# Moving two groups of SBUF tiles by 96 bytes, and reordering the products of the output projections

## The chip, the core and the metric

The program runs on one core of one Trainium2 chip, as one launch. The metric is the device time of that launch in microseconds (us), the median of several executions. One further execution is taken under the hardware profiler; all views of the profile come from that one, and the times in them count from the start of its span.

## What is computed

One layer of a transformer-like network on 256 tokens of width 2048, batch 1, all in 32-bit floats: a SwiGLU block, a token mixer, a second SwiGLU block. Each is entered through a layer norm modulated by an "ada" vector, and left through a gated residual and a layer norm:

```python
ada = (jax.nn.silu(c) @ w_ada + b_ada)[:, None, :]
sh1, sc1, g1, sh2, sc2, g2, sh3, sc3, g3 = jnp.split(ada, N_ADA, axis=-1)
h = _swiglu(_modulate(x, sh1, sc1), ffn1_w_in, ffn1_w_out)
x = _layernorm(ALPHA * x + 0.5 * (1 + g1) * h, ln1_g, ln1_b)
h = _token_mixer(_modulate(x, sh2, sc2), w_in, ...)
x = _layernorm(ALPHA * x + (1 + g2) * h, ln2_g, ln2_b)
h = _swiglu(_modulate(x, sh3, sc3), ffn2_w_in, ffn2_w_out)
x = _layernorm(ALPHA * x + 0.5 * (1 + g3) * h, ln3_g, ln3_b)
```

`_swiglu(h, w_in, w_out)` is `(silu(gate) * up) @ w_out` with 5632 features. The mixer multiplies its normalised rows by `w_in` (2048 by 6160), runs eight heads of softmax attention ("fox" heads) and four recurrent heads ("mLSTM"), joins their outputs to rows of width 2048, and multiplies these by its own `w_out`.

## The kernel before

**Products in parts.** Every large product is made of float32r matmuls. Both operands are split (`split`, lines L145 and L146): ScalarE (ACT) casts to a high part `hi`, and VectorE (DVE) subtracts to get a low part `lo`. Three matmuls then stand for one product: high by high, and the two mixed ones. Before the change they all come from `mm3` (L390 to L393). In the trace a matmul is named `out<-moving,stationary`: the stationary operand is loaded first (a weight load, engine row PEld), and then the moving operand streams past it.

**Two forms.** In form a (`cols_form_a`: tiles `s`, `gu_f`, `fh`, `fs`, `pr_m`, `pr_f`) the activations move, 256 columns at a time, and the weights are stationary. L391 and L392 use a weight's high part and L393 its low part. In form b (`mo`, `b_fv`, `b_mv`, `gf`, and the output projections `o_f` and `o_mx`) the weights move, mostly 512 columns at a time, and the activations are stationary: L391 high by high, L392 low weights, L393 low activations.

**Where the tiles lie.** Pools hand out SBUF by offset; a `gap` is a filler tile that does nothing but shift what is allocated after it. In the built program the operands of these matmuls start at these bytes of each partition, given modulo 512:

| operand | before | after |
|---|---|---|
| weights, high parts `hi` (six buffers) | 288 | 288 |
| weights, low parts `lo` (six buffers) | 160 | 160 |
| normalised rows of both SwiGLU blocks, `xhi_f`, `xlo_f` | 480 | 480 |
| normalised rows of the mixer, `xhi_mx`, `xlo_mx` | 384 | 480 |
| hidden rows of the SwiGLU output projections, `hh`, `hl` | 160 | 160 |
| fox heads' rows of the mixer's projection, `yhi`, `ylo` | 64 | 160 |
| mLSTM heads' rows of it, `yh`, `yl` | eight places | the same eight |

After the change `xhi_mx` has the same place as `xhi_f` modulo 8192 too, and `yhi` the same as `hh` modulo 2048.

**Output projections.** `out_proj` runs three times: for the two SwiGLU blocks (`o_f`, 44 row blocks) and for the mixer (`o_mx`, 16). It goes through the 2048 output columns in passes of 1024, 512 and 512, over all row blocks `k` in each, for two tiles of 128 tokens (`a`) and one or two banks of 512 columns (`b`). In the steady state each `k` comes from `load_w` as a pair `(hi, lo)` and is used at once. `held` and `kept` are row blocks whose products are put off to the end of a pass, so that the sums can be taken up by DVE (`add_up`) while PE works on the other token tile. The last four row blocks of the last pass run in halves of 256 columns (`last_products`).

**The order around it.** The tile framework orders each engine's instructions at build time. Beside the weight products it places the generators in `side`: the fox heads (L1075 to L1104) and the mLSTM heads, small chains that go from PE to DVE to ACT and back to PE. A weight goes DMA (issued on SyncE's queue) to `raw` (three buffers), ACT to `hi` (six buffers), DVE to `lo` (six buffers), PE. The ada rows arrive on the same queue and are summed by DVE (L158, L160), at rates set by `pump`.

Of the kernel before, what the change touches and what calls it, by code (L numbers as in the profile page):

```python
# [14 lines left out]
P = 128  # L15
# [32 lines left out]
def layer_kernel(  # L48
# [8 lines left out]
    V, S, G_, PE, SP = nc.vector, nc.scalar, nc.gpsimd, nc.tensor, nc.sync  # L57
# [5 lines left out]
    def gap(pool, nbytes, name):  # L63
        pool.tile([P, nbytes // 4], F32, tag=name, name=name)
# [325 lines left out]
    def mm3(o, ah, al, bh, bl, start, stop):  # L390
        PE.matmul(o, ah, bh, start=start, stop=False)  # L391
        PE.matmul(o, ah, bl, start=False, stop=False)  # L392
        return PE.matmul(o, al, bh, start=False, stop=stop)  # L393
# [28 lines left out]
    def out_proj(w, rows, nk, tag, npump, finish, before=None, turn=0, nheld=3, spare=None):  # L422
# [11 lines left out]
        for width in (1024, 512, 512):  # L434
            nb, kn = width // 512, 2048 // width
            nu = nk // kn
            ps = {(a, b): mm_tile(f"o_{tag}{col}{a}{b}") for b in range(nb) for a in range(2)}
            lastg = col + width == D
            held, kept, last, half = [], [], [], {}

            def products(a, args, k0=turn, k1=(turn - 1) % nk, outs=ps, c=0, w=512):
                ts_ = slice(a * P, (a + 1) * P)
                for k, hh, hl, hi, lo in args:
                    for b in range(nb):
                        bs = slice(b * 512 + c, b * 512 + c + w)
                        mm = mm3(outs[a, b][:, c:c + w], hh[:, ts_], hl[:, ts_], hi[:, bs], lo[:, bs],
                                 k == k0, k == k1)
                return mm


# [1 line left out]
            def last_products(a):  # L452
                half[a, 0] = mm_tile(f"oh_{tag}{a}")
                args = held[:-kn] + (kept if a else []) + held[-kn:]
                k0 = args[0][0] if a and kept and nu == nheld + 1 else None
                body, end = args[:-4], args[-4:]
                ends = end[0][0], end[-1][0]
                with tc.issue_after(last[0].ins) if a else nullcontext():
                    products(a, body, k0, None)
                    products(a, end, None, ends[1], w=256)  # L460
                    last.append(products(a, end, *ends, outs=half, c=256, w=256))


            def add_up(a, ps=ps, col=col, bs=range(nb), half=half):
# [17 lines left out]
            for i in range(nu):  # L482
                u = (i + turn // kn) % nu
                hs = []
                if before:
                    before(u * kn)
                if lastg and nu == 4 and i == nu - 1:
                    catch_up(4)
                keep = spare and lastg and i == nu - nheld - 1
                place, rows_ = spare() if keep else (None, rows)  # L490
                for k in range(u * kn, u * kn + kn, 2):
                    hs += rows_(k)
                for kk, hi, lo in load_w(w[u * kn * P:(u + 1) * kn * P, col:col + width], kn, width,
                                         f"{tag}o{col}_{u}", place):
                    arg = (u * kn + kk, *hs[kk], hi, lo)
                    if keep:
                        products(0, [arg])
                        kept.append(arg)
                    elif lastg and i >= nu - nheld or not lastg and i == nu - 1:
                        held.append(arg)  # L500
                    else:
                        for a in range(2):
                            products(a, [arg])
                if not lastg and i == nu - 1:

                    late += [add_up(a, bs=(b,)) for b in range(nb) for a in range(2)]
                    products(0, held)
                    catch_up(2)
                    products(1, held)
                elif nu > 4:  # L510
                    catch_up(2)
                elif not lastg:
                    catch_up(3)
                if not lastg or i < nu - 4:
                    npump()
# [180 lines left out]
    xp = tc.alloc_tile_pool(name="xp1", bufs=1, **right)  # L696
# [109 lines left out]
    held = {}  # L806
# [68 lines left out]
    for j in range(4):  # L875
        fa = next_ada(j + 1) if j < 3 else load_mixer_smalls()
        for n, i in enumerate(order_of(j)):
            w = list(ws if n + j == 0 else first_w(j, i))
# [8 lines left out]
    lnp = tc.alloc_tile_pool(name="ln1", bufs=1, **right)  # L887
# [17 lines left out]
    ent = {}  # L905

    def finish1(products, add_up, st):
        need(6)
        hp.release()
        ent["xp"] = tc.alloc_tile_pool(name="xp2", bufs=1)  # L910
        gap(ent["xp"], 544, "gap_x")
        ent["np"] = tc.alloc_tile_pool(name="np2", bufs=1)
        ent["f"] = (products, add_up, st)

# [30 lines left out]
    xp, npool = ent["xp"], ent["np"]  # L945
# [326 lines left out]
    for j in range(2):  # L1272
        ps = form_a_pair(C_MQ + j * 256, C_MK + j * 256, f"m{j}")
# [13 lines left out]
    for j in (2, 3, 0, 1):  # L1287
        ps = form_a_pair(C_FQ + j * 256, C_FK + j * 256, f"f{j}")
# [10 lines left out]
    lnp = tc.alloc_tile_pool(name="ln2", bufs=1)  # L1299
# [7 lines left out]
        if len(units) in (8, 12):  # L1307
            need(9 if len(units) == 8 else 10)

    gap(lnp, 224, "gap_y")  # L1310
    yhi, ylo = (lnp.tile([P, NFH, T], F32R, name=f"y{i}") for i in ("hi", "lo"))


# [42 lines left out]
    xp, npool = ent["xp"], ent["np"]  # L1356
# [33 lines left out]
    for j in range(2, 10):  # L1390
# [7 lines left out]
        ps = half_in(j, 0, "fh")  # L1398
# [82 lines left out]
```

## Time and profile before

| | |
|---|---|
| median of three executions | 1930.63 us (1930.4 to 1932.44) |
| the profiled execution, its own time | 1933.45 us |
| its span in the profile | 1931.8 us |
| granted TensorE clock | 0.998 of full speed |
| PE busy in the span | 1882.0 us |
| matmul records | 13109 |

The stages, one after another, from PE's instructions:

| stage | from, us | to, us |
|---|---|---|
| first SwiGLU, in-projection (`s`, `gu_f`) | 38.6 | 530.9 |
| its output projection (`o_f`) | 530.9 | 776.8 |
| mixer: output gates (`mo`) | 776.8 | 831.4 |
| mixer: values (`b_fv`, `b_mv`) | 831.4 | 902.6 |
| mixer: queries and keys (`pr_m`, `pr_f`) | 902.6 | 1059.3 |
| mixer: last values (`b_fv`) | 1059.3 | 1085.5 |
| mixer: output projection (`o_mx`) | 1085.5 | 1185.1 |
| second SwiGLU, in-projection | 1185.1 | 1678.7 |
| its output projection (`o_f`) | 1678.7 | 1931.8 |

A matmul's record has a start and a modelled end, and the records overlap: a matmul of 256 columns is listed with about 0.28 us and one of 512 with about 0.39 us, while the next one starts long before that. What a matmul costs is therefore read as the step from its start to the next start, over a run of matmuls with nothing else in between.

### The profile page before, as it was taken

The numbers are of one execution on the slowest core, as the hardware profiler recorded it, in microseconds if no ns is written. First come the engines' busy times: TensorE is split into PE (matmuls) and PEld (weight loads), VectorE is DVE, ScalarE is ACT, GpSimd is POOL, SyncE is SP. The second block draws the span as 40 slices with busy tenths as digits, with TensorE's granted clock in tenths as the row PEclk, the third lists the DMA queues.
The fourth block names the chain that finished last, engine by engine and source line by source line (L and its number), as shares of the span: only waits on it lengthen the run. The fifth ranks groups of instructions, "written<-read, shape, count | busy, mean of one in ns | idle before, by whom it ended". The sixth has DMA issues, their size and how long they took to land.

```text
span 1931.8 us, 32165 instructions
## 1 busy us (share of the span) xinstructions
PE 1882.0 (97%) x13109; PEld 1726.2 (89%) x13109; DVE 1466.0 (76%) x1774; ACT 931.4 (48%) x1296; POOL 54.2 (3%) x85
## 2 busy tenths in 40 slices
PE   3999999999999999999999999999999999999997
PEld 3999999999988888598999776999999999988886
DVE  7889979877778899678787787777775654555776
ACT  3554354444354464745664544555444444444562
POOL 1211100000000000000000000000000000000000
PEclk9999999999999999999999999999999999999999
DMA  9988969989799887489778784998777656655552
GB/s 354 356 312 304 332 209 315 327 297 335 267 336 315 274 302 259 154 311 318 266 252 288 282 296 147 324 313 270 236 260 257 226 196 197 228 189 193 196 195 89
DMA packets 295819, 510.89 MB, mean 264 GB/s; under 512 B 10834, under 2 KB 158962, under 8 KB 294648
## 3 DMA queue, kind: packets, MB, share of 16 engines
q1 hardware_dynamic: 287896, 480.53, 73.2%
q0 software_dynamic: 7776, 28.32, 4.2%
q8 instruction: 102, 1.67, 0.4%
q14 instruction: 45, 0.37, 0.1%
HBM read 506.71 MB, written 2.10 MB: 263 GB/s over the span
## 4 chain that ended last, share of the span: by engine, by line
PE 90%; DVE 5%; DMA 3%; ACT 1%; issue 1%; POOL 0%; SPq 0%; DVEq 0%; ACTq 0%; POOLq 0%
PE gu_f L391 8%; PE gu_f L393 8%; PE gu_f L392 8%; PE o_f L391 8%; PE o_f L393 8%; PE o_f L392 8%; PE s L391 4%; PE s L392 4%; PE s L393 4%; PE pr_f L393 2%; PE pr_f L392 2%; PE pr_f L391 2%; PE fh L393 2%; PE fh L392 2%; PE fh L391 2%; PE fs L392 1%
## 5 line engine op out<-in xcount | busy, mean ns | idle before, releaser
L160 DVE SCALAR_TENSOR_TENSOR acc<-ar,csil,acc 128x1024 f32<-128x1024 f32 x240 | 306.9, 1279 | 33.0 <-DMA ar<-in_w_ada_dram 32.6
L391 PE MATMUL s<-xhi_f,hi_s 128*128 128x256 f32 x768 | 213.3, 279 | 1.7 <-ACT xhi_f L325 0.9
L392 PE MATMUL s<-xlo_f,hi_s 128*128 128x256 f32 x768 | 213.0, 278 | 0.1
L393 PE MATMUL s<-xhi_f,lo_s 128*128 128x256 f32 x768 | 212.4, 277 | 0.0
L393 PE MATMUL gu_f<-xhi_f,lo_f2i 128*128 128x256 f32 x768 | 212.0, 276 | 0.0
L392 PE MATMUL gu_f<-xlo_f,hi_f2i 128*128 128x256 f32 x768 | 212.0, 276 | 0.0
L391 PE MATMUL gu_f<-xhi_f,hi_f2i 128*128 128x256 f32 x768 | 212.0, 276 | 0.0
L146 DVE TENSOR_TENSOR lo_f2i<-raw_f2i,hi_f2i 128x1024 fp32r<-128x1024 f32 x96 | 117.6, 1225 | 100.1 <-ACT hi_f2i L145 100.0
L391 PE MATMUL gu_f<-xhi_f,hi_f1i 128*128 128x256 f32 x640 | 176.8, 276 | 0.0
L393 PE MATMUL gu_f<-xhi_f,lo_f1i 128*128 128x256 f32 x640 | 176.7, 276 | 0.0
L392 PE MATMUL gu_f<-xlo_f,hi_f1i 128*128 128x256 f32 x640 | 176.7, 276 | 0.0
L145 ACT CAST hi_f2i<-raw_f2i 128x1024 fp32r<-128x1024 f32 x96 | 100.8, 1050 | 137.5 <-PE gu_f L392 125.5
L145 ACT CAST hi_s<-raw_s 128x1024 fp32r<-128x1024 f32 x96 | 100.2, 1053 | 114.0 <-PE s L392 86.8
L391 PEld LDWEIGHTS s<-xhi_f,hi_s 128*128 128x128 f32 x768 | 144.8, 189 | 2.0 <-ACT xhi_f L325 1.1
L392 PEld LDWEIGHTS s<-xlo_f,hi_s 128*128 128x128 f32 x768 | 145.0, 189 | 0.4 <-DVE xlo_f L327 0.3
L393 PEld LDWEIGHTS s<-xhi_f,lo_s 128*128 128x128 f32 x768 | 144.6, 189 | 0.3 <-DVE lo_s L146 0.3
L392 PEld LDWEIGHTS gu_f<-xlo_f,hi_f2i 128*128 128x128 f32 x768 | 144.2, 188 | 0.1
L391 PEld LDWEIGHTS gu_f<-xhi_f,hi_f2i 128*128 128x128 f32 x768 | 144.2, 188 | 0.1
L393 PEld LDWEIGHTS gu_f<-xhi_f,lo_f2i 128*128 128x128 f32 x768 | 144.2, 188 | 0.0
L145 ACT CAST hi_f1i<-raw_f1i 128x1024 fp32r<-128x1024 f32 x80 | 83.6, 1050 | 114.6 <-PE gu_f L392 80.3
L146 DVE TENSOR_TENSOR lo_f2o<-raw_f2o,hi_f2o 128x1024 fp32r<-128x1024 f32 x86 | 105.3, 1224 | 43.2 <-ACT hi_f2o L145 43.1
L145 ACT CAST hh<-hT 128x512 fp32r<-128x512 f32 x126 | 77.3, 620 | 114.1 <-PE o_f L392 113.8
(490 smaller groups left out, 5406.9 us busy)
## 6 DMA issues: line engine op xcount, KB each, us to landing
ar<-in_w_ada_dram SPq DMA_DIRECT2D x240, 512.0 KB, 5.9
raw_s<-in_ffn_w_in_dram SPq DMA_DIRECT2D x48, 1024.0 KB, 7.3
raw_f2i<-in_ffn_w_in_dram SPq DMA_DIRECT2D x48, 1024.0 KB, 5.1
raw_f1o<-in_ffn_w_out_dram SPq DMA_DIRECT2D x44, 1024.0 KB, 7.8
raw_f2o<-in_ffn_w_out_dram SPq DMA_DIRECT2D x44, 1024.0 KB, 5.1
raw_f1i<-in_ffn_w_in_dram SPq DMA_DIRECT2D x40, 1024.0 KB, 7.7
ar<-in_w_ada_dram POOLq DMA_DIRECT2D x48, 512.0 KB, 6.9
raw_mxo<-in_w_out_dram SPq DMA_DIRECT2D x16, 1024.0 KB, 8.1
```

The costliest lines, as they stand in the source:

```text
L145: S.copy(hi, src)
L146: V.tensor_tensor(out=lo, in0=src, in1=hi.bitcast(F32), op=ALU.subtract)
L160: ins = V.scalar_tensor_tensor(out=acc, in0=raw, scalar=csil[:, k:k + 1], in1=acc, op0=ALU.mult, op1=ALU.add)
L391: PE.matmul(o, ah, bh, start=start, stop=False)
L392: PE.matmul(o, ah, bl, start=False, stop=False)
L393: return PE.matmul(o, al, bh, start=False, stop=stop)
```

## The change

Two fillers grow by 96 bytes each, which moves what is allocated behind them: `gap_x` moves the mixer's normalised rows (and the small tiles of the entry to the mixer, `np2`) from 384 to 480 modulo 512, and `gap_y` moves the fox heads' high and low rows from 64 to 160.

In `out_proj` the helper `products` no longer calls `mm3`. It takes the row blocks in pairs (in the steady state it is called with one at a time), issues for all token tiles and banks the two products that read the weights' high part, and only then the products that read the low part. Number and shapes of the matmuls are the same, 12996 in the program before and after.

```diff
-            def products(a, args, k0=turn, k1=(turn - 1) % nk, outs=ps, c=0, w=512):
-                ts_ = slice(a * P, (a + 1) * P)
-                for k, hh, hl, hi, lo in args:
-                    for b in range(nb):
-                        bs = slice(b * 512 + c, b * 512 + c + w)
-                        mm = mm3(outs[a, b][:, c:c + w], hh[:, ts_], hl[:, ts_], hi[:, bs], lo[:, bs],
-                                 k == k0, k == k1)
+            def products(tiles, args, k0=turn, k1=(turn - 1) % nk, outs=ps, c=0, w=512):
+                for i in range(0, len(args), 2):
+                    each = [(arg, a, slice(a * P, (a + 1) * P), b, slice(b * 512 + c, b * 512 + c + w))
+                            for arg in args[i:i + 2] for a in tiles for b in range(nb)]
+                    for (k, hh, hl, hi, lo), a, ts_, b, bs in each:
+                        o = outs[a, b][:, c:c + w]
+                        PE.matmul(o, hh[:, ts_], hi[:, bs], start=k == k0, stop=False)
+                        PE.matmul(o, hl[:, ts_], hi[:, bs], start=False, stop=False)
+                    for (k, hh, hl, hi, lo), a, ts_, b, bs in each:
+                        mm = PE.matmul(outs[a, b][:, c:c + w], hh[:, ts_], lo[:, bs], start=False, stop=k == k1)
                 return mm
...
-                        for a in range(2):
-                            products(a, [arg])
+                        products((0, 1), [arg])
...
-        gap(ent["xp"], 544, "gap_x")
+        gap(ent["xp"], 640, "gap_x")
...
-    gap(lnp, 224, "gap_y")
+    gap(lnp, 320, "gap_y")
```

The other calls of `products` change only in that `a` becomes `(a,)`.

The first place to look at is PE in the steady state of the first SwiGLU's output projection: one row block `k`, with its weights `hi_f1o_10` and `lo_f1o_10`, the rows `hh` and `hl`, and the four sums `o_f_6136` to `o_f_6139`. Before:

```order
L391 MATMUL o_f_6136<-hi_f1o_10_6186,hh_6180 128x512
L392 MATMUL o_f_6136<-lo_f1o_10_6187,hh_6180 128x512
L393 MATMUL o_f_6136<-hi_f1o_10_6186,hl_6181 128x512
L391 MATMUL o_f_6138<-hi_f1o_10_6186,hh_6180 128x512
L392 MATMUL o_f_6138<-lo_f1o_10_6187,hh_6180 128x512
L393 MATMUL o_f_6138<-hi_f1o_10_6186,hl_6181 128x512
```

The other two sums follow in the same way. After the change, PE at the same place, the whole row block:

```order
L447 MATMUL o_f_6136<-hi_f1o_10_6186,hh_6180 128x512
L448 MATMUL o_f_6136<-hi_f1o_10_6186,hl_6181 128x512
L447 MATMUL o_f_6138<-hi_f1o_10_6186,hh_6180 128x512
L448 MATMUL o_f_6138<-hi_f1o_10_6186,hl_6181 128x512
L447 MATMUL o_f_6137<-hi_f1o_10_6186,hh_6180 128x512
L448 MATMUL o_f_6137<-hi_f1o_10_6186,hl_6181 128x512
L447 MATMUL o_f_6139<-hi_f1o_10_6186,hh_6180 128x512
L448 MATMUL o_f_6139<-hi_f1o_10_6186,hl_6181 128x512
L450 MATMUL o_f_6136<-lo_f1o_10_6187,hh_6180 128x512
L450 MATMUL o_f_6138<-lo_f1o_10_6187,hh_6180 128x512
L450 MATMUL o_f_6137<-lo_f1o_10_6187,hh_6180 128x512
L450 MATMUL o_f_6139<-lo_f1o_10_6187,hh_6180 128x512
```

The four products with the low part have moved behind the eight with the high part; a matmul with `hi` is now mostly followed by another with the same `hi`, and one with `lo` by another with the same `lo`.

The second place is PE at the start of the mixer's output projection. `lps1` are logits of fox head 1 (the second of a pair of heads handled there), `ptp0` is the transpose of the softmax `s0` of head 0, and `yhi` and `ylo` are the first row block's parts. Before:

```order
L1078 MATMUL lps1_11488<-qs1_10980 128x256
L391 MATMUL o_mx000_11519<-hi_mxo0_20_11527,yhi_11515 128x512
L392 MATMUL o_mx000_11519<-lo_mxo0_20_11528,yhi_11515 128x512
L391 MATMUL o_mx001_11521<-hi_mxo0_20_11527,yhi_11515 128x512
L392 MATMUL o_mx001_11521<-lo_mxo0_20_11528,yhi_11515 128x512
L391 MATMUL o_mx010_11520<-hi_mxo0_20_11527,yhi_11515 128x512
L392 MATMUL o_mx010_11520<-lo_mxo0_20_11528,yhi_11515 128x512
L391 MATMUL o_mx011_11522<-hi_mxo0_20_11527,yhi_11515 128x512
L392 MATMUL o_mx011_11522<-lo_mxo0_20_11528,yhi_11515 128x512
L1093 MATMUL ptp0_11560<-ident_79,s0_11473 128x128
L393 MATMUL o_mx000_11519<-hi_mxo0_20_11527,ylo_11516 128x512
L393 MATMUL o_mx001_11521<-hi_mxo0_20_11527,ylo_11516 128x512
```

After:

```order
L1080 MATMUL lps1_11488<-qs1_10980 128x256
L447 MATMUL o_mx000_11519<-hi_mxo0_20_11527,yhi_11515 128x512
L447 MATMUL o_mx001_11521<-hi_mxo0_20_11527,yhi_11515 128x512
L447 MATMUL o_mx010_11520<-hi_mxo0_20_11527,yhi_11515 128x512
L447 MATMUL o_mx011_11522<-hi_mxo0_20_11527,yhi_11515 128x512
L1095 MATMUL ptp0_11560<-ident_79,s0_11473 128x128
L448 MATMUL o_mx000_11519<-hi_mxo0_20_11527,ylo_11516 128x512
L448 MATMUL o_mx001_11521<-hi_mxo0_20_11527,ylo_11516 128x512
L448 MATMUL o_mx010_11520<-hi_mxo0_20_11527,ylo_11516 128x512
L448 MATMUL o_mx011_11522<-hi_mxo0_20_11527,ylo_11516 128x512
L450 MATMUL o_mx000_11519<-lo_mxo0_20_11528,yhi_11515 128x512
L450 MATMUL o_mx001_11521<-lo_mxo0_20_11528,yhi_11515 128x512
```

The four products with `lo_mxo0_20` stood between the logits and the transpose `ptp0`, and now stand behind it: four products are left in that place where there were eight. Elsewhere the order of PE changes only among the projections' own products. On ACT and DVE some casts and subtractions of `hh` and `hl` in the output projections come one place later among those of the weights, and two loads on SyncE's queue change places with ada rows.

More of the change, by code (lines that the diff above doesn't have):

```diff
@@ L458, in last_products @@
                 with tc.issue_after(last[0].ins) if a else nullcontext():
-                    products(a, body, k0, None)
-                    products(a, end, None, ends[1], w=256)
-                    last.append(products(a, end, *ends, outs=half, c=256, w=256))
+                    products((a,), body, k0, None)
+                    products((a,), end, None, ends[1], w=256)
+                    last.append(products((a,), end, *ends, outs=half, c=256, w=256))
             def add_up(a, ps=ps, col=col, bs=range(nb), half=half):
@@ L496, in out_proj @@
                     if keep:
-                        products(0, [arg])
+                        products((0,), [arg])
                         kept.append(arg)
@@ L501, in out_proj @@
                     else:
-                        for a in range(2):
-                            products(a, [arg])
+                        products((0, 1), [arg])
                 if not lastg and i == nu - 1:
                     late += [add_up(a, bs=(b,)) for b in range(nb) for a in range(2)]
-                    products(0, held)
+                    products((0,), held)
                     catch_up(2)
-                    products(1, held)
+                    products((1,), held)
                 elif nu > 4:
```

## The prediction

> **What bounds the kernel now.** I read the page first: busy times, the granted clock, the chain that ended last.
>
> ```profile
> span 1931.8 us, 32165 instructions
> PE 1882.0 (97%) x13109; PEld 1726.2 (89%) x13109; DVE 1466.0 (76%) x1774; ACT 931.4 (48%) x1296; POOL 54.2 (3%) x85
> PEclk9999999999999999999999999999999999999999
> PE 90%; DVE 5%; DMA 3%; ACT 1%; issue 1%; POOL 0%; SPq 0%; DVEq 0%; ACTq 0%; POOLq 0%
> ```
>
> PE is busy for 97% of the span, at full clock in every slice, and carries 90% of the chain. It hardly waits, so the change must be priced by what one matmul takes. The number and shapes of the matmuls stay as they are; what can change is the step from one matmul's start to the next. The second view is therefore PE's timeline. I took runs of matmuls with nothing else between them, and divide the distance from the first start to the last by the number of steps. First the form with 256 moving columns, at one place that the change leaves alone and at two that it moves:
>
> ```profile
> 1427.39 0.28 PE L391 MATMUL gu_f<-xhi_f,hi_f2i 128*128 128x256 f32 x1
> ...
> 1574.21 0.28 PE L393 MATMUL gu_f<-xhi_f,lo_f2i 128*128 128x256 f32 x1
> 998.62 0.47 PE L391 MATMUL pr_f<-xhi_mx,hi_f3b 128*128 128x256 f32 x1
> ...
> 1015.65 0.28 PE L393 MATMUL pr_f<-xhi_mx,lo_f0a 128*128 128x256 f32 x1
> ...
> 1046.16 0.37 PE L391 MATMUL pr_f<-xhi_mx,hi_f1b 128*128 128x256 f32 x1
> ...
> 1057.72 0.28 PE L393 MATMUL pr_f<-xhi_mx,lo_f1b 128*128 128x256 f32 x1
> ```
>
> `gu_f` makes 1295 steps in 146.82 us, 113.4 ns each. `pr_f` makes 143 in 17.03 us and 95 in 11.56 us, 119.1 and 121.7 ns, 120.1 together. Shapes, types and weight places (288 and 160 modulo 512) are equal; the moving rows lie at 480 in `gu_f` and at 384 in `pr_f`. A step is thus 6.7 ns dearer in `pr_f`, and placement is one reason that fits. Next the form in which the weights move and the rows are stationary:
>
> ```profile
> 831.57 0.28 PE L391 MATMUL b_fv<-hi_fv,xhi_mx 128*128 128x256 f32 x1
> ...
> 854.62 0.28 PE L391 MATMUL b_mv<-hi_mv,xhi_mx 128*128 128x256 f32 x1
> ...
> 878.53 0.40 PE L391 MATMUL b_mv<-hi_mv,xhi_mx 128*128 128x512 f32 x1
> ...
> 889.40 0.39 PE L393 MATMUL b_mv<-hi_mv,xlo_mx 128*128 128x512 f32 x1
> ...
> 1072.67 0.48 PE L391 MATMUL b_fv<-hi_fv,xhi_mx 128*128 128x512 f32 x1
> ...
> 1083.82 0.40 PE L393 MATMUL b_fv<-hi_fv,xlo_mx 128*128 128x512 f32 x1
> ...
> 1304.23 0.39 PE L391 MATMUL gf<-hi_gu,xhi_f 128*128 128x512 f32 x1
> ...
> 1315.06 0.39 PE L393 MATMUL gf<-hi_gu,xlo_f 128*128 128x512 f32 x1
> ```
>
> The narrow `b_fv` run makes 192 steps in 23.05 us, 120.0 ns. The wide runs make 47 steps each: 231.3 ns (`b_mv`), 237.2 (`b_fv`), and 230.4 in `gf`, whose stationary rows lie at 480. Last the output projections, and one row block of them in steady state:
>
> ```profile
> 703.28 0.39 PE L391 MATMUL o_f<-hi_f1o,hh 128*128 128x512 f32 x1
> 703.52 0.39 PE L392 MATMUL o_f<-lo_f1o,hh 128*128 128x512 f32 x1
> 703.74 0.39 PE L393 MATMUL o_f<-hi_f1o,hl 128*128 128x512 f32 x1
> 703.97 0.39 PE L391 MATMUL o_f<-hi_f1o,hh 128*128 128x512 f32 x1
> ...
> 1128.17 0.48 PE L391 MATMUL o_mx<-hi_mxo,yhi 128*128 128x512 f32 x1
> ...
> 1169.92 0.40 PE L393 MATMUL o_mx<-hi_mxo,yl 128*128 128x512 f32 x1
> ...
> 1678.67 0.39 PE L391 MATMUL o_f<-hi_f2o,h 128*128 128x512 f32 x1
> ...
> 1906.47 0.39 PE L393 MATMUL o_f<-hi_f2o,hl 128*128 128x512 f32 x1
> ```
>
> `o_mx` makes 179 steps in 41.75 us, 233.2 ns; `o_f`, with its rows at 160, makes 995 in 227.80 us, 228.9 ns. Within `o_f` the steps that begin at L391, L392 and L393 read 0.24, 0.22 and 0.23 us above; averaged by line over those 995 steps I get 232, 226 and 228 ns.
>
> Is it the place of the tiles, or the work beside them? The windows view gives, behind each engine's busy time and count, the granted clock, the DMA engines' share and GB/s:
>
> ```profile
> 310.40:530.90 220.50, 220.50 (x1939) 220.16 (x1938) 170.88 (x167) 91.54 (x103) 0.00 (x0) 1.00 0.92 307
> 831.40:902.60 71.20, 71.20 (x503) 66.35 (x502) 56.64 (x86) 34.52 (x58) 0.00 (x0) 1.00 0.92 316
> 902.60:1059.30 156.70, 155.93 (x1261) 154.03 (x1260) 123.98 (x187) 89.07 (x157) 1.65 (x1) 1.00 0.81 271
> ```
>
> In the first SwiGLU, whose rows have the good place, DMA share is 0.92 and DVE busy 77% of the time; in the query and key stage DMA share is 0.81 and DVE 79%. Load alone doesn't separate them. I choose the place.
>
> **The change, part by part.** The sum is made against the profiled execution, 1933.45 us (span 1931.8 and 1.65 around it), and its difference is carried to the median of 1930.63.
>
> Mixer rows to 480, form a: 1152 matmuls (`pr_m`, `pr_f`) should go from 120.1 to 113.4 ns: 1152 × 6.7 = **−7.7 us**. The bounds are nothing and the whole, since the same two shapes at the place of `xhi_f` show 113.4.
>
> Mixer rows to 480, form b, 512 wide: 312 matmuls (192 in the `b_` tiles, 120 in `mo`) go from the mean of the two runs, 234.3, to `gf`'s 230.4: 312 × 3.8 = **−1.2 us**. Bounds: 312 × 0.9 = 0.3 from `b_mv`, 312 × 6.8 = 2.1 from `b_fv`.
>
> The same, 256 or 264 wide: 384 matmuls. No row shows this form with rows at 480. One bound is nothing; the other is 384 × (120.0 − 113.4) = 2.5. I take half of the wide form's gain, 1.9 ns, as half the columns pass: **−0.7 us**.
>
> Fox rows to 160: 168 wide matmuls of `o_mx` use `yhi` or `ylo`; from 233.2 to `o_f`'s 228.9: 168 × 4.3 = **−0.7 us**. The other 192 keep their places.
>
> New order of products: 2424 wide products (2064 in `o_f`, 360 in `o_mx`). Streams of `hi` and of `lo` keep their numbers, two to one; at (232 + 228)/2 and 226 ns the sum is the same. What before doesn't show is `lo` behind `lo`, and `hi` behind `hi` at the place where L448 follows L447. If every step became the cheapest, 226, it would gain 2424 × 2.9 = 7.0; if every one became 232, it would lose 2424 × 3.1 = 7.5. I take the sum unchanged, **0**.
>
> The start of `o_mx`:
>
> ```profile
> 1085.54 0.58 PE L391 MATMUL o_mx<-hi_mxo,yhi 128*128 128x512 f32 x1
> ...
> 1086.42 0.40 PE L392 MATMUL o_mx<-lo_mxo,yhi 128*128 128x512 f32 x1
> ...
> 1087.35 0.40 PE L392 MATMUL o_mx<-lo_mxo,yhi 128*128 128x512 f32 x1
> 1087.65 0.40 ACT L1088 ACTIVATE s<-s,nm 128x128 f32<-128x128 f32 x1
> 1088.10 0.33 PE L1093 MATMUL ptp<-ident,s 128*128 128x128 f32 x1 [0.35 <-ACT s L1088]
> 1088.64 0.73 PE L393 MATMUL o_mx<-hi_mxo,ylo 128*128 128x512 f32 x2 [0.21 <-DVE ylo L146]
> ```
>
> `ptp0` waits for ACT's `s`, which ends at 1088.05. Eight products stood ahead of it; four will, so PE arrives four products earlier and waits for the same end, and the four are done later instead: 4 × 0.233 = **+0.9 us**. Behind it in PE's queue stand the products with `ylo`, which wait until 1088.6 in any case. ACT and DVE have the same order here, so nothing moves `s`.
>
> Covers that get thinner: a faster PE asks for weights sooner. The thinnest in the moved stages:
>
> ```profile
> 1038.10 1.23 DVE L146 TENSOR_TENSOR lo_f1a<-raw_f1a,hi_f1a 128x1024 fp32r<-128x1024 f32 x1 [0.77 <-ACT hi_f1a L145]
> ...
> 1039.52 0.28 PE L393 MATMUL pr_f<-xhi_mx,lo_f1a 128*128 128x256 f32 x1
> ```
>
> `lo_f1a` is ready at 1039.33, 0.19 us before its use. Weights come six buffers ahead and their loads follow when buffers come free, so a faster PE pulls the loads with it; still I charge **+0.2 us** for this place. The later casts of `hh` and `hl`, and the loads of row blocks 13 and 14 that change places with ada rows, are costed at nothing, by this row of the page:
>
> ```profile
> L145 ACT CAST hh<-hT 128x512 fp32r<-128x512 f32 x126 | 77.3, 620 | 114.1 <-PE o_f L392 113.8
> ```
>
> ACT was idle for 113.8 us ahead of these casts because PE had not yet given buffers back: they run ahead of PE, and one place later among ACT's casts (about 1 us) hides there. Without that cover each microsecond would cost one.
>
> Sum: −7.7 − 1.2 − 0.7 − 0.7 + 0 + 0.9 + 0.2 = **−9.2 us**: 1924.3 profiled, **1921.4** in the median.
>
> The Trainium skill, page "SBUF — State Buffer", section "Who interferes with whom", says that PE and ACT never wait on anyone, and the section "A bandwidth-pool intuition that's wrong (but worth ruling out)" gives weight loads a second, independent read port. By these a tile's place could cost PE nothing, and the first four terms would be 0. The trace doesn't bear that out as far as equal shapes go (113.4 against 120.1 ns), though it doesn't say why they differ.
>
> **The rivals.** Place doesn't decide; the mixer's side work does. For it: fox and mLSTM chains run beside `pr_f`. Against it: the narrow `b_fv` run has little of them and still takes 120.0. Then only the start of `o_mx` is left: 1930.63 + 0.9 = 1931.5. This is also the case in which the fillers don't do what they are there for, and the one that the page's rule would give.
>
> Supply eats half of the mixer's gain: the lead of 0.19 us at `lo_f1a`, on DVE at 79%, becomes a wait at each weight. Against it: DMA share would go from 0.81 to about 0.81 × 120.1/113.4 = 0.86, and 0.92 was sustained at 113.4 ns. About 4.6 of the 9.2 would go: 1926.0.
>
> The new order helps: if a matmul is cheaper when the next one reads the same weight tile, all 2424 go to 226: another −7.0, about 1914.5. For it: only that one of the three steps is at 226 already, and no row says why. Against it: from L393 to L391 of the next bank's pair the moving rows and the stationary tile both change, and at 228 that step is no dearer than the average of 228.9.
>
> The new order hurts, the case on the other side: two matmuls in a row that load different rows against the same `hi`, eight deep, might cost what the worst wide run does, 237.2. Then 2424 × 8.3 = +20.1: about 1941. It takes away the 9.2 at 9.2/2424 = 3.8 ns a product (232.7), and the kernel is slower by 0.2% (3.9 us) from 13.1/2424 = 5.4 ns on (234.3). For it: the step behind L391 is the dearest of the three, and such steps stay; against it: L393 to L391 is already a pair within `hi`, at 228.
>
> **How the numbers follow.** A measurement of this kernel can tell about 0.2%, 3.9 us, from no change, so faster ends at 1926.8 and slower begins at 1934.5. Forecast 0.60, by itself 1917 to 1925 from the bounds of the 256-wide term (−1.8, +0.7), the wide terms (±0.9) and a drift of the order term by a quarter of its bounds (±1.8). Supply 0.10 (0.08 faster, 0.02 same). Order helps 0.12, faster. Place doesn't decide 0.09, same. Order hurts 0.09: slower 0.05, and same 0.04, where it eats just the gain. Faster 0.80, same 0.15, slower 0.05. The range from 1914.5 to 1928.0 takes in forecast, supply and most of the case in which the order helps.
>
> **What would show it.** Right: `pr_f` at 113 to 114 ns a step, `gf`-like 230 to 231 in the wide `b_` runs, `o_mx` with `yhi` at 229, `o_f` still at 229, and 1.4 to 1.5 us of PE's wait at `ptp0`. Wrong: `pr_f` still near 120 (place), or the hidden order term: `o_f` at 226 or beyond 232 moves the time by more than all the mixer does. New rows `pr_f <- lo` among PE's waits would mean supply.

## The result, and the profile after

The changed kernel takes **1936.47 us** in the median of 20 executions (1931.39 to 1938.99), the kernel before 1931.59 us in the median of 20 (1929.55 to 1933.95). The ratio is 1.0022, 95% interval 1.0016 to 1.0028: by the ratio the change is slower by some 4.2 us (the two medians lie 4.9 us apart), where 1921.4 had been forecast. Of all the executions told of below, one stands apart, with 4700.49 us, of the version with the new order in `o_f` alone; that version's ratio leaves it out.

First the page of the changed kernel, its span and busy times (as in the prediction):

```profile
span 1934.4 us, 32126 instructions
PE 1882.4 (97%) x13109; PEld 1721.4 (89%) x13109; DVE 1462.7 (76%) x1774; ACT 931.8 (48%) x1296; POOL 54.1 (3%) x85
```

The busy times say nothing: PE is busy for 0.4 us more, out of 2.6 us by which the span grew. The stages say more. This table gives, from the starts of PE's first instructions, how long each took in the profiled execution, for both kernels and for three versions that are told of below (`ge` are the first products of the second SwiGLU block):

| stage, us | before | change | places only | order only | one head's transposes a step |
|---|---|---|---|---|---|
| first `o_f` | 245.8 | 248.5 | 245.6 | 248.5 | 245.6 |
| `mo`, first values | 125.8 | 125.2 | 125.0 | 125.2 | 125.2 |
| queries and keys | 156.7 | 151.7 | 152.9 | 157.8 | 154.7 |
| last values | 26.2 | 25.8 | 25.8 | 26.2 | 26.0 |
| `o_mx` up to `ge` | 99.5 | 103.5 | 99.1 | 100.6 | 95.4 |
| second in-projection | 493.6 | 493.6 | 493.6 | 493.6 | 493.6 |
| second `o_f`, to the end | 253.1 | 255.8 | 253.1 | 255.8 | 253.1 |

The mixer did gain where its rows were moved: 0.6 + 5.0 + 0.4 = 6.0 us (though most of the 0.6 stands in the version with the order only as well, where no tile moved). Both SwiGLU projections lost, 2.7 and 2.8 us before rounding, and the mixer's own projection lost 3.9. Ahead of the first `o_f`, where the program is the same, this execution of the changed kernel was 0.7 us faster. Together that makes the 2.6 us.

PE's timeline of the changed kernel, the same runs of matmuls as in the prediction, first and last row of each (a row with x2 stands for two matmuls, and its start is that of the first):

```profile
996.12 0.47 PE L391 MATMUL pr_f<-xhi_mx,hi_f3b 128*128 128x256 f32 x1
...
1012.55 0.28 PE L393 MATMUL pr_f<-xhi_mx,lo_f0a 128*128 128x256 f32 x1
...
1043.22 0.36 PE L391 MATMUL pr_f<-xhi_mx,hi_f1b 128*128 128x256 f32 x1
...
1054.09 0.28 PE L393 MATMUL pr_f<-xhi_mx,lo_f1b 128*128 128x256 f32 x1
...
1678.52 0.39 PE L447 MATMUL o_f<-hi_f2o,h 128*128 128x512 f32 x1
...
1908.82 0.63 PE L450 MATMUL o_f<-lo_f2o,hh 128*128 128x512 f32 x2
```

The two runs of `pr_f`, 143 and 95 steps, take 16.43 and 10.87 us: 114.7 ns a step, where it was 120.1. The run of `o_f` takes 230.30 us in 994 steps: 231.7 ns, where it was 228.9. Over 2064 products this is 5.8 us.

At the start of `o_mx`, four products now stand between the logits and `ptp0`:

```profile
1081.44 1.28 PE L447 MATMUL o_mx<-hi_mxo,yhi 128*128 128x512 f32 x4
1083.97 0.40 ACT L1090 ACTIVATE s<-s,nm 128x128 f32<-128x128 f32 x1 [0.25 <-DVE nm L1089]
1084.42 0.33 PE L1095 MATMUL ptp<-ident,s 128*128 128x128 f32 x1 [1.70 <-ACT s L1090]
1085.47 1.05 PE L448 MATMUL o_mx<-hi_mxo,ylo 128*128 128x512 f32 x2
1086.32 0.63 PE L448 MATMUL o_mx<-hi_mxo,ylo 128*128 128x512 f32 x1
1086.75 0.63 PE L450 MATMUL o_mx<-lo_mxo,yhi 128*128 128x512 f32 x1
1087.60 1.04 PE L450 MATMUL o_mx<-lo_mxo,yhi 128*128 128x512 f32 x2
```

The fourth product starts at 1082.33 and is through some 0.23 us later; `ptp0` starts at 1084.42. PE stands still for 1.86 us (1.70 by the trace, which counts from the matmul's modelled end), against 0.52 before. Then something that the prediction did not have: the next products follow each other at 0.43 us, not 0.23. The windows view of the same kernel, with the granted clock third from the right, shows why:

```profile
1081.40:1084.40 3.00, 1.32 (x6) 0.76 (x4) 3.00 (x12) 2.75 (x8) 0.00 (x0) 1.00 0.89 285
1084.40:1088.40 4.00, 3.77 (x9) 2.86 (x10) 3.57 (x6) 2.95 (x8) 0.00 (x0) 0.59 1.00 418
1088.40:1092.40 4.00, 4.00 (x21) 3.27 (x20) 1.99 (x2) 1.79 (x4) 0.00 (x0) 0.99 0.86 293
```

For 4 us behind the wait the granted clock is 0.59 on average; the trace has it at half for 3.41 us. Eight products at 0.43 instead of 0.23 us cost 1.6 us, more than the 1.34 us by which the wait grew. And the faster query and key stage runs into waits of its own; the waits view of the changed kernel (total, times, longest, in us) against that of before:

```profile
PE ptp L1095 <- ACT s L1090: 3.2, 3, 1.7
PE ytp L1246 <- DVE gate L217: 1.8, 1, 1.8
PE nps L1210 <- DVE dm L1205: 0.5, 1, 0.5
```

```profile
PE ptp L1093 <- ACT s L1088: 1.4, 2, 1.0
PE ytp L1244 <- DVE gate L217: 0.8, 1, 0.8
```

`ytp` are the transposes of the mLSTM heads' outputs; they wait 1.0 us longer than before, and `nps` waits 0.5 us, which it did not.

### The profile page after: what moved, and what is told of

Its sections match the earlier page's. It is cut to its first block, busy times and chain, and to the rows that moved or that the text cites. A ratio compares the mean times of both kernels' runs of the same rounds, so it can differ in the third digit from the quotient of the medians.

```text
span 1934.4 us, 32126 instructions
## 1 busy us (share of the span) xinstructions
PE 1882.4 (97%) x13109; PEld 1721.4 (89%) x13109; DVE 1462.7 (76%) x1774; ACT 931.8 (48%) x1296; POOL 54.1 (3%) x85
## 4 chain that ended last, share of the span: by engine, by line
PE 82%; issue 10%; DVE 4%; DMA 2%; ACT 1%; POOL 0%; DVEq 0%; SPq 0%; POOLq 0%; ACTq 0%
PE gu_f L391 8%; PE gu_f L393 8%; PE gu_f L392 8%; PE o_f L447 8%; PE o_f L450 8%; PE o_f L448 8%; PE s L393 5%; PE s L391 5%; PE s L392 5%; PE fh L391 2%; PE fh L392 2%; PE fh L393 1%; PE fs L393 1%; PE fs L392 1%; PE fs L391 1%
## 5 line engine op out<-in xcount | busy, mean ns | idle before, releaser
L145 ACT CAST hi_f2o<-raw_f2o 128x1024 fp32r<-128x1024 f32 x86 | 90.1, 1049 | 111.0 <-PE o_f L448 96.5
L145 ACT CAST hi_f1o<-raw_f1o 128x1024 fp32r<-128x1024 f32 x86 | 89.2, 1049 | 106.3 <-PE o_f L448 51.6
```

What stands on the lines that cost most here:

```text
L145: S.copy(hi, src)
```

## The experiments

All ratios are to the kernel before, timed beside the runs. For the experiments `products` was written so that each projection can have an order of its own. `hh` is high rows by high weights, `hl` high rows by low weights, `lh` low rows by high weights (here these are names of products, not of tiles); `e` lists the token tiles and banks of one call. `old` is the order of before and `new` that of the change:

```python
orders = {
    'old': lambda e: [(t, x) for x in e for t in ('hh', 'hl', 'lh')],
    'new': lambda e: [(t, x) for x in e for t in ('hh', 'lh')] + [('hl', x) for x in e],
    'triple': lambda e: [(t, x) for x in e for t in ('hh', 'lh', 'hl')],
    'lofirst': lambda e: [('hl', x) for x in e] + [(t, x) for x in e for t in ('hh', 'lh')],
    'swap': lambda e: [(t, x) for x in e for t in ('lh', 'hh')] + [('hl', x) for x in e],
    'by_part': lambda e: [('hh', x) for x in e] + [('lh', x) for x in e] + [('hl', x) for x in e],
    'mixed': lambda e: [(t, x) for x in e for t in ('hh', 'hl')] + [('lh', x) for x in e],
}
```

Theory A was: the places gain what the mixer's stages show, the new order loses in all three projections, in the mixer's by the wait and the clock. Four versions take the change apart.

**The places alone.** Fillers 640 and 320, all projections `old`.

> Only the two fillers are changed (640 and 320 bytes); the products keep the order of before. Theory A (the places gain, the order of products loses): the mixer up to the start of o_mx stays as short as in the changed kernel, pr_f at about 113.8 ns a step, o_f back at 228.9 ns, o_mx back at about 86 us; in all 6 to 7 us under before's 1931.6, that is 1924.5 to 1925.5. Rival B (the new place of the fox rows, not the order, made o_mx 3.9 us longer): o_mx stays near 90 us and the time is about 1929.

1927.85 against 1932.70 us: 0.9977 (0.9966 to 0.9987), some 4.5 us faster. The steps of `o_f` are as expected, 228.9 ns in the second projection; the long runs of `pr_f` take 114.4 to 116.1 ns, where 113.8 was expected. `o_mx` up to `ge` takes 99.1 us, so rival B falls. The gain is 2 us smaller than expected, and the waits view has 1.8 of them in one row (0.8 us before):

```profile
PE ytp L1262 <- DVE gate L217: 2.6, 1, 2.6
```

**The order alone.** Fillers 544 and 224, all projections `new`.

> Only the order of products is changed; both fillers are as before (544 and 224 bytes). Theory A: o_f at 231.8 ns a step in both SwiGLU blocks (+5.5 us), o_mx 1 to 4 us longer by a longer wait of ptp0, pr_f at 119 to 120 ns; about 1938 to 1941. Rival C (the dearer step of o_f needs the new places): o_f at 228.9 and the time within 2 us of before plus the wait at ptp0, 1932 to 1935.

1939.87 against 1932.70 us: 1.0035 (1.0021 to 1.0048). Both `o_f` are as slow as with the change (the table's first and last rows), with no tile moved; rival C falls. `o_mx` took 1.1 us longer, and the clock did not fall in this profile.

**The new order in one kind of projection.** Fillers as in the change; first `{'mx': 'old'}` with the rest `new`, then `{'f1': 'old', 'f2': 'old'}` with the mixer's `new`.

> The changed kernel with the order of before in the mixer's projection alone; both SwiGLU projections keep the new order. Theory A: o_f at 231.8 ns, o_mx back at about 86 us with the clock at 1.00 behind ptp0; 3.9 us under the changed kernel, about 1932.5. Rival B: o_mx stays near 90 us, about 1936.5.

> The changed kernel with the order of before in both SwiGLU projections; the mixer's keeps the new order. Theory A: o_f back at 228.9 ns (5.5 us less), ptp0 waits some 1.7 us and the granted clock falls to about half for some 3.5 us behind it in most executions; about 1930 to 1931, with single executions 2 us or more lower where the clock does not fall. Rival B': the clock falls for another reason than the wait (the streak of eight products with one moving tile), then it falls in all executions alike.

With the new order in both `o_f`: 1933.58 us, 1.0005 (0.9996 to 1.0014), 5.7 us over the places alone. With it in `o_mx` only: 1930.03 us, 0.9985 (0.9976 to 0.9994), 2.2 over them. Theory A wanted 5.5 us for the first difference, and the second kernel's time is the one that it gave (1930 to 1931); the first kernel is 1.1 us over the 1932.5 expected. One expectation failed: in the second, the clock did not fall at `ptp0`, which waited 1.2 us there, but behind `ytp`, which waited 2.8 us (windows view, before and behind the end of that wait):

```profile
1010.00:1015.00 5.00, 2.15 (x16) 1.70 (x15) 3.97 (x5) 2.36 (x3) 0.00 (x0) 1.00 1.08 367
1015.00:1020.00 5.00, 5.00 (x33) 5.00 (x31) 4.21 (x7) 1.43 (x3) 0.00 (x0) 0.66 1.08 376
```

So the fall doesn't belong to the new order. Any place where PE waits some two microseconds can have it, in one execution and not in the next; what decides it is shown below, under the change again.

**Which part of the order costs.** New places; `{'f1': 'triple', 'f2': 'lofirst', 'mx': 'mixed'}`, then `{'f1': 'swap', 'f2': 'by_part', 'mx': 'old'}`.

> New places; three orders in one kernel. First SwiGLU: per sum high by high, low rows by high weights, high rows by low weights. Second SwiGLU: all products with the low weights first, then those with the high weights. Mixer: per sum high by high and low weights, then all with low rows. Theory P (a step's length goes by the part that streams and the part of the rows that is loaded under it, with the means of the changed kernel: 234.7, 229 and 229.9 in the first case): o_f 231.2 ns in the first SwiGLU, 231.7 in the second. Rival Q (runs of four with the low weights are what costs): 228.9 in the first, 231.8 in the second. Mixer: eight products that need no low rows stand ahead of ptp0 again, so by theory A its wait is 0.5 to 1 us, without a fall of the clock there, and o_mx about 86 us.

> New places, mixer in the order of before. First SwiGLU: as in the change, but low rows ahead of high rows in each pair with the high weights. Second SwiGLU: all high by high, then all low rows by high weights, then all with the low weights. Theory P: 231.5 ns in the first, 232.7 in the second. Rival Q: 231.8 in both, since both have the runs of four.

The times are 1930.84 us (0.9992, 0.9983 to 1.0001) and 1934.00 us (1.001, 1.0001 to 1.0019). The steps decide. The first kernel's first `o_f` (`triple`), over 335 steps without a break:

```profile
574.55 0.48 PE L466 MATMUL o_f<-hi_f1o,hh 128*128 128x512 f32 x1
...
651.33 0.39 PE L466 MATMUL o_f<-lo_f1o,hh 128*128 128x512 f32 x1
```

76.78 us, 229.2 ns: the step of before in the same run of products (229.1). Averaged over the whole projections, without the few steps in which other work stands, `lofirst` gives 232.0, `swap` 231.9, `by_part` 231.7. Theory P falls (it wanted 231.2 for `triple`, 232.7 for `by_part`), and the numbers are those of rival Q.

Rival Q's cause, the four products with the low weights in a row, falls all the same. Such streaks, with streaks of eight high products between them, exist only in the pass over 1024 columns. In the passes over 512 columns one bank is open, and the new order has two low products and four high ones in a row. Its steps are as dear there: in the second `o_f` of the changed kernel 231.7 ns in the first pass and 231.9 in the second, where the kernel before has 229.0 and 228.9. Nor is `triple` a test of pairs: in the order of before, too, two products with the high weights follow each other, the last of one sum and the first of the next, so both orders give PE the same cycle of parts, two high and one low.

The traces can be sorted by the weights' part of a product and of the next one. These are the steps of the 512 columns wide products in the second `o_f` (number, mean in ns; the row blocks put off to the end of a pass and one or two steps with other work in them are left out):

| order | high to high | high to low | low to low | low to high |
|---|---|---|---|---|
| before | 333 at 228.5 | 336 at 232.4 | none | 336 at 226.0 |
| change | 548 at 232.5 | 124 at 229.2 | 212 at 232.4 | 121 at 230.0 |
| `lofirst` | 548 at 232.3 | 121 at 230.3 | 212 at 232.5 | 123 at 232.1 |
| `by_part` | 546 at 232.4 | 124 at 229.4 | 212 at 232.4 | 121 at 230.0 |

Low to low takes 232.4 ns, and high to high has gone from 228.5 to 232.5. As the latter are many more, they make up 2.0 of the 2.8 us that the change loses in this projection against 228.9 ns a step, and low to low 0.7. Every dear order has both, longer streaks of high products and streaks of low ones, and no run has the one without the other. In the mixer (`mixed`) eight products stand ahead of `ptp0` again, and the wait is 0.4 us, with the clock at full.

**Other places for the hidden rows.** `{'f1': 'new', 'f2': 'old', 'mx': 'old'}` and both fillers `gap_h` from 320 to 448. The pool of these rows grows from the other end of SBUF, so they lie at 32 modulo 512 in the built program, not at the 288 that the expectation names.

> New places, mixer in the order of before; the hidden rows of both SwiGLU projections lie at 288 modulo 512 instead of 160. First SwiGLU in the new order, second in the order of before. If the dearer step of the new order comes of where rows and weights lie to each other, the first moves from 231.8 ns by over 1 ns, and the second away from 228.9 as well. If it is the order alone, 231.8 and 228.9 stay.

1934.24 us, 1.0009 (0.9999 to 1.0018). First the new order in the first projection, 334 steps, then the order of before in the second, 995 steps:

```profile
579.17 0.48 PE L466 MATMUL o_f<-hi_f1o,hh 128*128 128x512 f32 x1
...
655.90 0.63 PE L466 MATMUL o_f<-lo_f1o,hh 128*128 128x512 f32 x2
...
1675.89 0.39 PE L466 MATMUL o_f<-hi_f2o,h 128*128 128x512 f32 x1
...
1907.88 0.39 PE L466 MATMUL o_f<-hi_f2o,hl 128*128 128x512 f32 x1
```

229.7 ns for the new order and 233.2 for the old. At 160 the new order took 232.5 ns in the same run of the first projection (334 steps of the changed kernel), and the old one 228.9 in that of the second: at 32 the ranking of the two orders is turned round. Over the whole first projection the new order takes 230.3 ns at 32 and 231.9 at 160. Sorted as above, the steps from high to high have come down most, from 232.4 to 229.6 ns; those from low to low are at 231.8 instead of 232.3. So the price of an order isn't a property of the order; it belongs to the order and the place together. (This kernel also waited 2.4 us at the start of the first `o_f`, and the clock was at 0.63 behind it.)

**The wait in the query and key stage.** Behind PE's transposes `ytp` of head 0 stood those of head 1; between them, in the version with the places only (timeline, all engines):

```profile
1010.51 0.39 PE L180 MATMUL bc<-alo,trir 128*128 128x512 f32 x1
1010.75 0.60 PE L1262 MATMUL ytp<-ident,og 128*128 128x128 f32 x4
...
1012.02 1.23 DVE L146 TENSOR_TENSOR lo_f1a<-raw_f1a,hi_f1a 128x1024 fp32r<-128x1024 f32 x1 [0.73 <-ACT hi_f1a L145]
1012.84 0.47 ACT L1268 ACTIVATE yh<-ytp,hcol 128x256 fp32r<-128x256 f32 x1
1013.16 1.28 DVE L217 SCALAR_TENSOR_TENSOR gate<-bc,gate 128x512 f32<-128x512 f32 x2
1013.90 0.66 PE L1262 MATMUL ytp<-ident,og 128*128 128x128 f32 x4 [2.56 <-DVE gate L217]
```

The second set waits until DVE's L217 has read `bc` out of PSUM, and L217 stands in DVE's queue behind `lo_f1a`, which waits for ACT. A faster PE comes to this place earlier, and DVE does not. Two versions move transposes, both with the new places and `old` everywhere. The first puts one `yield` more into each head:

```diff
                                    in1=o, op0=ALU.mult, op1=ALU.mult)
         yield
+        yield
         yp = aux_tile(f"ytp{h}")
```

> New places and the order of before, and in each mLSTM head's output one more step of the side work between DVE's products and PE's transposes (ytp), which puts the transposes of heads 0 and 1 behind another 48 products. Theory D (what the faster mixer gives back is the wait of ytp for DVE's gate work, L217, and in part of the executions the clock that falls behind it): the wait of 2.6 us goes, the stage pr_f0 takes 26 us instead of 28.1, the time is about 2 us under the version with the places only, 6.5 us under before, and the executions differ less. Rival: the wait moves to the next transposes or to pr_f1, and the time is that of the version with the places only, 4.5 us under before.

1927.51 against 1932.25 us, 0.9975 (0.9966 to 0.9984): no better than the places alone. The rival came true: the waits moved to the transposes of heads 2 and 3 and the logits behind them (1.0 us at `ytp`, 1.4 at `lps`, with 0.6 us of transposes between), and the clock fell there. The second version holds back every other head only:

```diff
         yield
+        if h in (1, 3):
+            yield
         yp = aux_tile(f"ytp{h}")
```

> New places and the order of before; in the output of mLSTM heads 1 and 3 one more step between DVE's products and PE's transposes, so that only one head's transposes come in the place in which PE waited for two. Theory D' (the wait is for the one PSUM tile that DVE's gate work still reads, so that one set of transposes can pass and the other cannot): the wait of 1.8 to 2.8 us at ytp goes, pr_f0 takes about 26 us, and the time is 1 to 2 us under the version with the places only. Rival: as with both sets moved, the wait goes on to the transposes of heads 2 and 3, and nothing is won.

**1924.97** against 1932.23 us, 0.9963 (0.9950 to 0.9975), five executions between 1924.23 and 1926.51. Its waits view has no `ytp` any more, and no low clock in the mixer:

```profile
PE ptp L1111 <- ACT s L1106: 0.6, 1, 0.6
PE nps L1226 <- DVE dm L1221: 0.5, 1, 0.5
```

It beats both the kernel before and the changed one. Over the version with the places only it gains 2.9 us by the medians, but the two intervals overlap. The gain doesn't stand in the stage that was named: queries and keys took 154.7 us, not 152.9 or less, and `o_mx` up to `ge` 95.4 instead of 99.1; together 250.1 against 251.9. Side work has moved from the one to the other: in the first stage PE has 115 matmuls of it instead of 108, in the second 38 instead of 46. And the sign of short supply that the prediction had named is there:

```profile
PE pr_f L393 <- DVE lo_f0a L146: 0.6, 1, 0.6
PE pr_f L393 <- DVE lo_f1a L146: 0.5, 1, 0.5
PE pr_f L391 <- ACT hi_f1a L145: 0.4, 1, 0.4
```

**Filling the wait.** The changed kernel, with the four products high by high of the first row block of `o_mx` issued twice, ahead of `ptp0`:

```diff
+                    if tag == 'mx' and col == 0 and each[0][0][0] == k0:
+                        plan = [('fill', x) for x in each] + plan
...
+                        if what == 'fill':
+                            PE.matmul(o, hh[:, ts_], hi[:, bs], start=True, stop=True)
+                            continue
```

> The changed kernel with four matmuls more: in the first row block of the mixer's projection the four products high by high are issued twice, ahead of ptp0, and the second time starts the sums anew. They are 0.93 us of work in a place where PE waits 1.9 us. If the wait is what lets the clock fall (theory A), it shrinks to about 0.9 us, the granted clock stays at 1.00 behind ptp0, o_mx takes about 88.2 us instead of 89.9, and the kernel is no slower than the changed one (about 1935). If the clock falls for another reason, it falls here too and o_mx stays at 89.9; if the wait follows the work ahead of it, the kernel is 0.9 us slower.

1935.45 us, 1.0018 (1.0009 to 1.0027): no slower than the change with four matmuls more. `ptp` waited 0.5 us, the clock stayed at 1.00 there, and `o_mx` up to the products of its last half (`oh_mx`) took 85.6 us instead of 89.9, better than the 88.2 expected. In this profile the clock fell behind `ytp`, which waited 2.7 us.

**The change again**, one execution:

> The changed kernel once more, for a second profile of it. If the clock's fall depends on when the wait comes (single executions lay between 1931.4 and 1939.0), the steps and waits are the same to 0.2 us and the places with a low clock can differ: at ptp0, at ytp, at both or at neither, some 1.6 us for each. If it belongs to the kernel, the clock falls behind ptp0 and nowhere else.

1935.42 us, span 1932.2, 2.1 us below that of the first profile. The waits are not the same to 0.2 us: `ytp` waits 2.8 us (1.8 in the first profile) and `ptp0` 1.3 (1.7). The clock falls at neither, although the wait at `ytp` is a long one.

The traces show what decides it. In all of them the granted clock changes only at whole multiples of 3.413 us, counted from the moment at which it first became full, and each of the seven falls within a kernel lasts one such stretch. So cut PE's time into these stretches (windows view; behind the length come PE's busy time and its matmuls, and the clock is third from the right). First the change's first profile, around `ptp0`, then this one, around `ytp`:

```profile
1081.66:1085.08 3.42, 1.51 (x7) 1.00 0.97 325
1085.08:1088.49 3.41, 3.41 (x9) 0.50 0.99 416
...
1011.99:1015.41 3.42, 2.17 (x16) 1.00 1.09 361
1015.41:1018.82 3.41, 1.82 (x16) 1.00 1.07 371
1018.82:1022.23 3.41, 3.41 (x32) 1.00 1.07 382
```

The wait of 2.8 us lies across a border, and neither stretch is idle enough. In the 14 traces together, the clock is at half behind every stretch in which PE was busy for 1.5 us or less (seven within the kernels, and the one at each kernel's end), and behind no stretch in which it was busy for 1.56 us or more. Whether a wait of two microseconds costs the clock therefore depends on where it falls between two borders, and within a kernel that is luck.

**Three other places at once.** The faster version above with `gap_x` 608, and `gap_h` 384 in the first SwiGLU and 576 in the second. In the built program that puts the mixer's rows at 448 and the hidden rows at 96 and 416.

> The version with one head's transposes a step, in the order of before, with three other places: the mixer's rows at 448 modulo 512 instead of 480, the hidden rows at 96 in the first SwiGLU projection and at 416 in the second instead of 160. Theory E (a step's length is set by where rows and weights lie, for one shape and one order): pr_f leaves 113.8 ns, and the two o_f leave 228.9 ns and differ from each other by over 1 ns. Rival: only 384 was a bad place and only the order counts in the projections: pr_f stays at 113.8, o_f at 228.9 in both.

1930.61 us against 1933.51 for before, one execution each. Timeline: the run of 143 steps in `pr_f`, and 995 steps of the second `o_f`:

```profile
998.67 0.47 PE L391 MATMUL pr_f<-xhi_mx,hi_f3b 128*128 128x256 f32 x1
...
1015.70 0.28 PE L393 MATMUL pr_f<-xhi_mx,lo_f0a 128*128 128x256 f32 x1
...
1675.83 0.39 PE L466 MATMUL o_f<-hi_f2o,h 128*128 128x512 f32 x1
...
1903.62 0.39 PE L466 MATMUL o_f<-hi_f2o,hl 128*128 128x512 f32 x1
```

At 448 `pr_f` is back at 119.1 ns, as at 384 before, against 114.9 at 480 in the same run of the changed kernel. At 416 `o_f` takes 228.9 ns, as at 160; at 96 its first projection takes 231.1, averaged over the whole of it, where 160 gives 229.0. Theory E holds for the mixer's rows and for 96; 416, which lies 256 bytes from 160, makes no difference at all, so there the rival is right.

## Why the prediction was wrong

The forecast was −9.2 us and the change is at about +4.2; on the profiles, −9.2 against +2.6. By the steps of the prediction:

- **Form a, −7.7.** What the term rests on held: the rows' place sets the step. Moved alone they give 114 to 116 ns in these runs, and at 448 it is 119.1 again. The size was off: over the same two runs 120.1 became 114.7, that is 1152 × 5.4 = 6.2 us. The price of `gu_f` was right, as without the first step of each run the changed kernel takes 113.5 ns. The 120.1 was not comparable with it: it holds the first step behind side work, 308 and 207 ns in the two runs, and the new place leaves that as it is (306 and 201). The stage kept 5.0 of the gain.
- **Form b, −1.2 and −0.7.** The last values gained 0.4, the wide first values (`b_mv`, 24.1 to 23.9 us) 0.2; what else the stage of `mo` shows comes with the order only too. The 256 and 264 columns wide products kept their 23.0 and 23.9 us to the tenth, so that term is 0, the end of its range. Of the wide ones, the 237.2 ns of `b_fv` held a first step of 315 ns behind side work, as the 120.1 above. Some 0.6 us instead of 1.9.
- **Fox rows, −0.7.** About 0.4 in the version with the places only (`o_mx` up to `ge` 99.1 instead of 99.5); under the new order next to nothing (100.4 us in the second profile of the change, 100.6 with the order only, both with 2.2 us of waits at `ptp`).
- **New order, 0. This is the step that failed**, for 5.5 us: "Streams of `hi` and of `lo` keep their numbers, two to one … the sum is the same." The three means, 232, 226 and 228 ns, were taken as prices of the single products. They are steps in one fixed cycle of three, and don't carry over to another sequence: behind one of its own kind a product with the low weights starts after 232 ns, and one with the high weights after 232 to 233 instead of 228.5, while the fewer changes between the two parts are at 229 and 230. The mean is 231.7 instead of 228.9. The order alone (248.5 and 255.8 us in both projections, with no tile moved) and the order in `o_f` alone (5.7 us) show that the order is the cause; whether the longer streaks of high products or those of low ones do it is not shown. The rival "new order hurts" had the direction, with a chance of 0.09. The steps that it named, several deep against the same `hi`, did get dearer, to 232.5 ns and not to the 237.2 that it charged; the steps from low to low it did not have, and its reason, different rows loaded against the same weights, is not shown either.
- **Start of `o_mx`, +0.9.** The wait was seen, its size not: PE stood still 1.34 us longer than before, not 0.93, as the softmax chain itself came later against PE. Behind it came 1.6 us lost at half the clock in the first profile, which is the luck of that execution. The stage lost 3.9; of the remaining 1.0, half is a longer wait at the transposes of the second pair of heads (1.5 us in all, 1.0 before).
- **Thin covers, +0.2.** The lead at `lo_f1a` held, the place was wrong. What a faster PE met first was the chain of the side work, at `ytp` and `nps`: 1.5 us longer waits in the changed kernel, 2.5 with the places only, and a clock that may fall behind. That DVE has one queue for weights and side work, and that the page showed 0.8 us of wait at `ytp` already, was there to be read.

The rival by which place doesn't decide is refuted: in the version with the places alone the steps of `pr_f` changed with no instruction moved. What stays open is why the steps depend on place and order. The runs show that they do, that 256 bytes make no difference in the one pair tried, and that the ranking of two orders turns with the place; no run shows the mechanism.

## What to carry to other kernels

A step time read from a timeline holds for its sequence of matmuls and for the places of its tiles; before an order is changed, measure the new sequence by itself, and try an order and a place together, since each can turn the other's sign. When an engine at 97% gets faster in one stage, look at once at where it next waits for a chain that hasn't got faster, above all for one that it hits twice in a row. And count a wait of PE of about two microseconds as more than its length, because the clock may be halved behind it; two shorter waits close together can add up to the same.

## What the runs showed of the hardware

- **Place of tiles.** The same matmuls, 143 of them in a row with the same work around them, took 119.1 ns a step with the moving rows at 384, 114.9 at 480 and 119.1 at 448 modulo 512. For 512 columns, with the weights at 288 and 160, in the order of before: rows at 160 or 416 228.9 ns, at 32 233.2 (second `o_f`), at 96 231.1 (first `o_f`, 229.0 at 160). The Trainium skill, page "SBUF — State Buffer", section "Who interferes with whom", has PE wait on nobody; it speaks of the engines beside it and not of places, and these runs differ by place alone.
- **Order of products.** With the rows at 160, moving tiles in the cycle of two high parts and one low took 228.9 to 229.0 ns a step, and longer streaks of each part (eight and four, or four and two) 231.7 to 232.0, each over a whole projection. With the rows at 32 it was 233.2 (995 steps of the second `o_f`) and 230.3 (the first).
- **The clock.** The granted clock changed only at multiples of 3.413 us from its first full moment. Behind a stretch of that length in which PE was busy for 1.5 us or less it was at half for the next one, and a product of 512 columns then took 0.43 us; behind a stretch with 1.56 us or more it stayed full. Counted by waits, those of 1.7 to 1.8 us cost the clock once in five cases (at `ptp0`, in the first profile), those of 2.4 to 2.8 us in five of seven, single ones of 1.3 us and less never, and two of 1.0 and 1.4 us close together did. A fall costs some 1.6 us. The Trainium skill, page "TensorE: Matmul & The Clock Gate", section "Part 1: The HAM clock gate", gives the half rate, a free-running window of about 3.4 us and an idle window of that length as its condition; the half rate and the window agree with the traces, but here a window in which PE stood idle for little over half was enough.
